# Small half-array matmuls of a group issued in one piece, and gated linear attention with two states

## The chip, the cores and the metric

The kernel runs on 1 core of one Trainium2 chip. TensorE (PE in the views) multiplies matrices from SBUF into banks of PSUM, VectorE (DVE) and ScalarE (ACT) work on SBUF and PSUM, GpSimd (POOL) on SBUF, and SyncE (SP) issues transfers. The metric is the time of one execution on the device, in microseconds.

## The reference, cut to what matters

Four post-norm blocks, whose mixer is chunked softmax attention (layers 0 and 3, 16 heads of 64), gated linear attention (layer 1) and differential attention (layer 2), each followed by a SwiGLU feed-forward network; then a second network with a feed-forward part, a mixer of top-k attention, a short convolution and gates, a memory cross-attention and another feed-forward part. 256 tokens, width 1024, float32. The change touches the products of queries and keys, and this part of the gated linear attention (chunks of 64 tokens, 4 heads, a state of 128 x 256 for each):

```
chunk_kv = jnp.einsum('bnchk,bnchv->bnhkv', k_dec, v)
chunk_decay = jnp.exp(total[:, :, 0]).astype(chunk_kv.dtype)

def step(state, inp):
    dec, kv = inp
    state = dec[..., None] * state + kv
    return state, state
...
_, states = lax.scan(step, init, (jnp.moveaxis(chunk_decay, 1, 0), jnp.moveaxis(chunk_kv, 1, 0)))
o = jnp.einsum('bnchk,nbhkv->bnchv', q, states)
```

## The kernel before

The 256 tokens are two token tiles of 128. Each tile is a generator (`stream`) that goes through the whole network; `run` interleaves the two, tile 1 some quarters of a weight unit behind tile 0. Weights (345 MB) come from DRAM in the order of use, in quarters, and each quarter is split by ScalarE (L268) and VectorE (L269) into two float32r halves, `wh` and `wl`. A product of activations and weights is then three float32r matmuls of 128 x 512 for each row tile (`mm3`, L280, L282, L284, into banks `lin` or `acc`). These are called ordinary matmuls below. Both tiles use the same quarters, so that one tile's weight matmuls can stand on TensorE where the other waits.

The small products are plain float32 matmuls, each of which the trace shows as two records. Some of them use half of the array:

- L574 in `attn_probs`: scores of four heads with 64 features each. Heads with e = 0 lie on partitions 0 to 63 and write to the first of two `at` banks, those with e = 1 lie on partitions 64 to 127 and write to the second. Tile 0 has 128 keys (128 columns), tile 1 has 256. Two such groups ("sub" 0 and 1) belong to each call of the loop over g, 14 groups to each tile in all.
- L842 in `mixer2`: index scores, in the same way; eight matmuls for tile 0, two groups of four for tile 1.
- L741 in `mixer_gla`: keys times values for each chunk c of 64 tokens (partitions 64c and up) and head x of a pair, into `at` bank c.
- L753 in `mixer_gla`: queries of chunk c times the state; 128 rows of the array but 64 columns, so that chunk 0 uses one half of the columns and chunk 1 the other; both write to one bank `lin`.

Behind an L574 group VectorE forms four maxima with the bias (L580), ScalarE four exponentials (L585), TensorE transposes them (L599) into `at` banks, and copies (L606, L608) free these. There are only two `at` banks; all transposes of activations (L326) pass through them too. The state S of the linear attention is one tile, updated in place by VectorE (L749 for the first chunk, L751 then).

The order of issue on each engine is not that of the code. `order_issue` plays the instructions through a list scheduler (`plan_order`, `play`) with assumed durations (`_duration`) and deadlines, and hands the order that it found to the framework as edges; waits follow from the data. So any change of the program gives a new order for all engines.

Of the kernel before, what the change touches and what calls it, by code (L numbers as in the profile page):

```python
# [15 lines left out]
OP = mybir.AluOpType  # L16
# [12 lines left out]
TW = 384          # length of a Toeplitz table  # L29
TREP = 32         # copies of a table in DRAM, for the skewed reads  # L30

LAG = 6           # quarters of a weight unit by which token tile 1 trails token tile 0
LAG0, LAGK = 2, 4   # the lag starts at LAG0 and grows by one every LAGK quarters
WB, RB = 10, 5    # buffers for split and for raw weight quarters
DMAQ = 1          # quarters of 1024 floats in one transfer
AHEAD = 1         # quarters split ahead of token tile 0


# [1 line left out]
# A unit is (key, kind, source, spec). kind "in": eight row tiles of the listed column ranges;  # L40
# kind "out": up to four row tiles of all 1024 columns.
# [74 lines left out]
class Unit:  # L116
    def __init__(self, key, kind, width, nrt):
        self.key, self.kind, self.width, self.nrt = key, kind, width, nrt
        self.cols = nrt * width                      # floats of a partition
        self.per = 2 if kind == "in" else 1          # row tiles of a quarter  # L120
        if kind == "in" and width < 64:
            self.per = 8
        self.nq = nrt // self.per
        self.qcols = self.per * width
        self.dma_q = max(1, min(self.nq, 1024 * DMAQ // self.qcols))   # quarters of one transfer

# [17 lines left out]
def pack_weights(inputs):  # L144
    """The weights in the order of their use: a block for each transfer, whole per partition."""
# [22 lines left out]
def rel_bias_rows(inputs):  # L168
    """[layers, heads, 257], by ascending (key - query)."""
    return np.ascontiguousarray(np.asarray(inputs["a_rel_bias"])[:, ::-1, :].transpose(0, 2, 1))  # L170


# [31 lines left out]
def bcast(ap, n):  # L204
    """A row of n floats in DRAM, read by every partition."""
# [3 lines left out]
class Net:  # L209
    def __init__(self, ctx, tc, A, out):  # L210
# [12 lines left out]
        self.tag_of, self.bufs_of = {}, {}  # L223

    # ---- tiles
# [15 lines left out]

    def bank(self, tag):
        return self.named(self.ps, tag, [128, 512], F32, {"acc": 4, "lin": 2, "at": 2}[tag])

    # ---- weights
# [27 lines left out]
    def pieces(self, n):  # L273
        """The very first quarter comes in two pieces, so that the tensor engine starts on the first."""
# [11 lines left out]
    def lin(self, st, key):  # L286
        """A step for each quarter: [128 tokens, width] = x @ columns of the unit."""
# [12 lines left out]
    def lin_out(self, gt, key, accs, first, last):  # L300
        u = self.by_key[key]
        both = 0 if u is self.units[-1] else u.nq - 1 if last else u.nq       # the quarters that do both halves at once
# [18 lines left out]
    # ---- small pieces  # L321
    def transpose4(self, src, n=4):
        """[128, n*128] -> a bank with [128, n, 128], each block transposed."""
# [33 lines left out]
    # ---- set-up  # L357
# [18 lines left out]
    def setup_later(self):  # L376
# [12 lines left out]
        # w_g2 with b_g as one more row  # L389
# [16 lines left out]
    def setup_last(self):  # L406
# [9 lines left out]
        # -(e1 - e2 + init) = e2 - (e1 + init)  # L416
# [7 lines left out]
    def toeplitz(self, i, bank=None):  # L424
        """Copies of layer i's biases by (key - query), per head, in DRAM."""
# [13 lines left out]
    def bias_tile(self, i, h0):  # L439
        """[128 queries, 4 heads, 256 keys] of the Toeplitz bias, masked in its last block."""  # L440
# [14 lines left out]
    # ---- normalisation  # L455
# [31 lines left out]
    def inv_rms(self, ss, n, scale=1.0):  # L487
        """ss: sums of squares [128, m]; -> scale * rsqrt(ss / n + EPS)."""
# [11 lines left out]
    def inv_rms_row(self, halves, half=False):  # L500
        """rsqrt(mean of squares + EPS) over two halves of 512; times 0.5, as 4 under the root, for half."""
# [37 lines left out]
    # ---- feed-forward  # L539
# [24 lines left out]
    # ---- softmax attention for eight heads of 64, in pairs  # L564
    def attn_probs(self, tt, sub, qT, kT, bias):
        """Four heads (pairs 2*sub, 2*sub+1): unnormalised exponentials [128, 4, keys], 1/sums."""
        nc = self.nc
        nk = 128 * (tt + 1)
        banks = [self.bank("at").rearrange("p (a k) -> p a k", a=2) for _ in range(2)]
        for i in range(2):  # L570
# [19 lines left out]
    def transpose_probs(self, tt, P, hs):  # L590
        """P[:, h, keys] for h in hs -> [128 keys, len(hs), key tiles, 128 queries]."""
# [18 lines left out]
    def to_heads(self, tt, acc, dst, scale=1.0):  # L610
        """A bank [128 tokens, 512] -> dst [128 features, 4, 128 tokens]."""
# [77 lines left out]
    # ---- gated linear attention  # L689
    def mixer_gla(self, tt, st, i):  # L690
        nc = self.nc
        # gates: log_sigmoid((x W1) W2 + b), still times 16
# [35 lines left out]
        on = []  # L728
        if tt == 0:
            self.S = self.t("k4", [128, 1032], 2)[:, :1024].rearrange("p (a k) -> p a k", a=4)  # L730
        S = self.S
        for pr in range(2):
# [3 lines left out]
            banks = [self.bank("at").rearrange("p (a k) -> p a k", a=2) for _ in range(2)]  # L736
            for x in range(2):
                hd = 2 * pr + x
                for c in range(2):
                    cs = slice(64 * c, 64 * c + 64)  # L740
                    nc.tensor.matmul(banks[c][:, x], kd[cs, 128 * hd:128 * hd + 128], v[cs, 256 * x:256 * x + 256],  # L741
                                     start=True, stop=True)
            o = self.bank("lin")
            for c in range(2):
                cs = slice(64 * c, 64 * c + 64)
                for x in range(2):
                    hd = 2 * pr + x
                    if tt == 0 and c == 0:
                        nc.vector.tensor_copy(S[:, hd], banks[c][:, x])  # L749
                    else:  # L750
                        nc.vector.scalar_tensor_tensor(S[:, hd], S[:, hd], decay[:, 2 * hd + c:2 * hd + c + 1],  # L751
# [626 lines left out]
```

## Time and profile before

| | |
|---|---|
| median of 3 runs | 1971.57 us (1969.64 to 1972.45) |
| profiled execution, span | 1969.9 us |
| PE busy | 1945.0 us, 99% |
| DVE busy | 1169.3 us, 59% |
| ACT busy | 927.4 us, 47% |
| POOL busy | 48.6 us, 2% |
| mean transfer rate | 175 GB/s |
| granted TensorE clock, mean | 0.998 |

The profiled execution lies inside the range of the runs. Busy time of PE is the union of matmuls that overlap in its pipeline (an ordinary one lasts some 0.4 us, but the next starts earlier), so what a matmul occupies is read from the distance of starts. The stage of the linear attention's products lies at 370 to 421 us, those of the three softmax layers around 30 to 115, 665 to 750 and 978 to 1063 us, and the mixer of the second network at 1510 to 1575 us.

### The profile page before, as it was taken

The numbers are of one execution on the slowest core, as the hardware profiler recorded it, in microseconds if no ns is written. First come the engines' busy times: TensorE is split into PE (matmuls) and PEld (weight loads), VectorE is DVE, ScalarE is ACT, GpSimd is POOL, SyncE is SP. The second block draws the span as 40 slices with busy tenths as digits, with TensorE's granted clock in tenths as the row PEclk, the third lists the DMA queues.
The fourth block names the chain that finished last, engine by engine and source line by source line (L and its number), as shares of the span: only waits on it lengthen the run. The fifth ranks groups of instructions, "written<-read, shape, count | busy, mean of one in ns | idle before, by whom it ended". The sixth has DMA issues, their size and how long they took to land.

```text
span 1969.9 us, 23888 instructions
## 1 busy us (share of the span) xinstructions
PE 1945.0 (99%) x8998; PEld 1546.9 (79%) x8998; DVE 1169.3 (59%) x1687; ACT 927.4 (47%) x1332; POOL 48.6 (2%) x71
## 2 busy tenths in 40 slices
PE   8999999999999999999999999999999999999998
PEld 6788887678888777888877888878887788788886
DVE  5566456557555768545755655664467857556454
ACT  5445445444444555444554444444444545555442
POOL 0000000000000000000000000000001000000000
PEclk9999999999999999999999999999999999999999
DMA  9436555645555434655543655465545355536562
GB/s 287 150 139 209 181 191 154 193 148 198 186 183 182 171 129 162 222 183 181 183 143 135 217 186 184 150 225 181 186 171 183 113 197 193 163 116 206 180 186 70
DMA packets 103293, 345.59 MB, mean 175 GB/s; under 512 B 13369, under 2 KB 20473, under 8 KB 103178
## 3 DMA queue, kind: packets, MB, share of 16 engines
q1 hardware_dynamic: 103178, 344.07, 51.7%
q8 instruction: 70, 1.15, 0.2%
q14 instruction: 45, 0.37, 0.1%
HBM read 341.01 MB, written 3.01 MB: 175 GB/s over the span
## 4 chain that ended last, share of the span: by engine, by line
PE 95%; DMA 2%; DVE 1%; ACT 1%; issue 0%; SPq 0%; DVEq 0%; POOLq 0%; ACTq 0%
PE lin L282 19%; PE lin L280 19%; PE lin L284 19%; PE acc L282 9%; PE acc L284 9%; PE acc L280 9%; PE at L326 4%; PE at L574 2%; PE lin L662 1%; PE at L599 1%; DMA raw<-in_weights_dram 1%; DMA toep<-t 1%; PE lin L753 0%; PE at L741 0%; PE lin L951 0%; DVE wl L269 0%
## 5 line engine op out<-in xcount | busy, mean ns | idle before, releaser
L269 DVE TENSOR_TENSOR wl<-raw,wh 128x1024 fp32r<-128x1024 f32 (+2 forms) x614 | 741.8, 1216 | 459.6 <-ACT wh L268 459.0
L268 ACT ACTIVATE wh<-raw 128x1024 fp32r<-128x1024 f32 (+2 forms) x614 | 644.7, 1053 | 680.9 <-PE lin L284 437.6
L280 PE MATMUL lin<-wh,sth 128*128 128x512 f32 x1696 | 677.1, 403 | 3.2 <-ACT sth L331 1.4
L282 PE MATMUL lin<-wl,sth 128*128 128x512 f32 x1696 | 671.5, 400 | 1.7 <-DVE wl L269 1.7
L284 PE MATMUL lin<-wh,stl 128*128 128x512 f32 x1696 | 669.1, 399 | 0.0
L280 PEld LDWEIGHTS lin<-wh,sth 128*128 128x128 f32 x1696 | 319.5, 188 | 78.7 <-issue 4.0
L284 PEld LDWEIGHTS lin<-wh,stl 128*128 128x128 f32 x1696 | 319.3, 188 | 77.5 <-issue 4.9
L282 PEld LDWEIGHTS lin<-wl,sth 128*128 128x128 f32 x1696 | 319.4, 189 | 76.8 <-issue 4.8
L282 PE MATMUL acc<-wl,gth 128*128 128x512 f32 x752 | 251.7, 401 | 0.1
L280 PE MATMUL acc<-wh,gth 128*128 128x512 f32 x752 | 248.5, 399 | 0.2 <-ACT gth L331 0.2
L284 PE MATMUL acc<-wh,gtl 128*128 128x512 f32 x752 | 248.3, 398 | 0.0
L284 PEld LDWEIGHTS acc<-wh,gtl 128*128 128x128 f32 x752 | 141.2, 188 | 33.7 <-issue 1.3
L282 PEld LDWEIGHTS acc<-wl,gth 128*128 128x128 f32 x752 | 140.8, 189 | 32.5 <-issue 1.4
L280 PEld LDWEIGHTS acc<-wh,gth 128*128 128x128 f32 x752 | 139.8, 188 | 31.9 <-issue 1.0
L326 PE MATMUL at<-ident,t 128*128 128x128 f32 x604 | 100.4, 273 | 4.5 <-DVE t L534 1.5
L326 PEld LDWEIGHTS at<-ident,t 128*128 128x128 f32 x604 | 75.2, 140 | 28.3 <-ACT t L613 4.1
L331 ACT ACTIVATE gth<-at 128x512 fp32r<-128x512 f32 (+1 forms) x98 | 55.4, 566 | 65.8 <-PE at L326 65.7
L555 DVE TENSOR_TENSOR t<-t,lin 128x512 f32<-128x512 f32 x60 | 41.2, 687 | 74.7 <-PE lin L284 74.7
L347 POOL TENSOR_TENSOR sm<-sm,mhalf 128x1 f32<-128x1 f32 (+2 forms) x42 | 35.8, 852 | 1672.6 <-DVE sm L474 952.1
L332 DVE TENSOR_TENSOR gtl<-at,gth 128x512 fp32r<-128x512 f32 (+1 forms) x98 | 64.1, 654 | 20.2 <-ACT gth L331 17.0
L585 ACT ACTIVATE p<-p,sm 128x128 f32<-128x128 f32 (+1 forms) x112 | 49.6, 444 | 52.4 <-DVE sm L583 52.4
L552 ACT ACTIVATE t<-lin 128x512 f32<-128x512 f32 x60 | 35.9, 598 | 49.8 <-PE lin L284 49.5
(158 smaller groups left out, 911.2 us busy)
## 6 DMA issues: line engine op xcount, KB each, us to landing
raw<-in_weights_dram SPq DMA_DIRECT2D x607, 512.0 KB, 3.5
b<-toep SPq DMA_DIRECT2D x40, 128.0 KB, 4.1
bc<-in_ln_g_dram SPq DMA_DIRECT2D x8, 512.0 KB, 3.7
bc<-in_ln_b_dram SPq DMA_DIRECT2D x8, 512.0 KB, 5.9
toep<-t SPq DMA_DIRECT2D x2, 768.0 KB, 10.4
bc<-in_ffn_post_g_dram SPq DMA_DIRECT2D x2, 512.0 KB, 3.6
p<-in_mem_dram SPq DMA_DIRECT2D x2, 512.0 KB, 6.6
out_dram<-h SPq DMA_DIRECT2D x4, 256.0 KB, 2.0
```

What stands on the lines that cost most here:

```text
L268: nc.scalar.activation(hi[:, c], src[:, c], AF.Copy)
L269: nc.vector.tensor_sub(lo[:, c], src[:, c], hi[:, c].bitcast(F32))
L280: nc.tensor.matmul(o, xh, w, start=first, stop=False)
L282: nc.tensor.matmul(o, xh, w, start=False, stop=False)
L284: nc.tensor.matmul(o, xl, w, start=False, stop=last)
L326: self.nc.tensor.transpose(b[:, k], src[:, k * 128:(k + 1) * 128], self.ident)
L331: self.nc.scalar.activation(hi, b[:, :n], AF.Copy)
L332: self.nc.vector.tensor_sub(lo, b[:, :n], hi.bitcast(F32))
L552: nc.scalar.activation(gate[j], acc, AF.Silu)
L555: nc.vector.tensor_mul(s, s, acc)
L574: nc.tensor.matmul(banks[e][:, i, :nk], qT[ps, pr, :], kT(ps, pr, nk), start=True, stop=True)
L585: nc.scalar.activation(P[:, hh, :nk], P[:, hh, :nk], AF.Exp, bias=nm[:, hh:hh + 1], accum_out=sm[:, hh:hh + 1])
```

## The change

Comments and docstrings are dropped, so that line numbers move (L574 becomes L581, L599 L606, L741 L750, L753 L766, L842 L856, L896 L910, L280, L282 and L284 become L286, L288 and L290). Two things change.

The first: the matmuls of a group are named as a burst. The planner makes the first of a burst wait for everything that any of them needs, all banks of the burst included, lets no other matmul in between, takes the least deadline of the group for all, and assumes a shorter duration for each. Within a group the loops of the code alternate the halves.

The second: the linear attention keeps two state tiles, S[0] for even and S[1] for odd chunks. VectorE writes S[c] from S[1 - c] instead of in place, all four updates of a pair of heads come first, and then the four matmuls with the queries as one burst.

```
+    def burst(self, *banks):
+        self.bursts.append([b.tensor.name for b in banks])
...
         banks = [self.bank("at").rearrange("p (a k) -> p a k", a=2) for _ in range(2)]
+        self.burst(*banks)
...
+            self.S = [self.t("k4", [128, 1032], 2)[:, :1024].rearrange("p (a k) -> p a k", a=4) for _ in range(2)]
...
+            for x in range(2):
+                hd = 2 * pr + x
+                for c in range(2):
+                    if tt == 0 and c == 0:
+                        nc.vector.tensor_copy(S[0][:, hd], banks[c][:, x])
+                    else:
+                        nc.vector.scalar_tensor_tensor(S[c][:, hd], S[1 - c][:, hd], decay[:, 2 * hd + c:2 * hd + c + 1],
+                                                       banks[c][:, x], op0=OP.mult, op1=OP.add)
             o = self.bank("lin")
-            for c in range(2):
-                cs = slice(64 * c, 64 * c + 64)
-                for x in range(2):
-                    hd = 2 * pr + x
-                    if tt == 0 and c == 0:
-                        nc.vector.tensor_copy(S[:, hd], banks[c][:, x])
-                    else:
-                        nc.vector.scalar_tensor_tensor(S[:, hd], S[:, hd], decay[:, 2 * hd + c:2 * hd + c + 1],
-                                                       banks[c][:, x], op0=OP.mult, op1=OP.add)
-                    nc.tensor.matmul(o[cs, 256 * x:256 * x + 256], qT[:, hd, cs], S[:, hd], start=True, stop=True)
+            self.burst(o)
+            for x in range(2):
+                hd = 2 * pr + x
+                for c in range(2):
+                    cs = slice(64 * c, 64 * c + 64)
+                    nc.tensor.matmul(o[cs, 256 * x:256 * x + 256], qT[:, hd, cs], S[c][:, hd], start=True, stop=True)
...
+        if burst:
+            rep = 2.4
         return rep * max(n / 2.4, 40.0) + 3
...
+    for names in bursts:
+        seq = sorted({i for name in names for i, _ in writers[name] if ops[i].eng == "PE"})
+        head = ops[seq[0]]
+        for i in seq:
+            op = ops[i]
+            op.burst = seq
+            op.dur = _duration(op.inst, op.eng, True)
+            if op is not head:
+                for j, full in op.preds.items():
+                    if j not in seq:
+                        assert j < head.idx
+                        head.preds[j] = max(full, head.preds.get(j, 0))
+                op.preds.setdefault(head.idx, 0)
+                head.opens += op.opens
+                op.opens = []
...
+        if op.burst and op.idx == op.burst[0]:
+            d = min(ops[i].dl for i in op.burst)
+            for i in op.burst:
+                ops[i].dl = d
...
+        if lock and op.eng == "PE" and op.idx != lock[0]:
+            return inf
...
+        if lock and e == "PE":
+            lock.pop(0)
+        elif op.burst:
+            lock = op.burst[1:]
```

TensorE's order in the linear attention, tile 0, first pair of heads, before:

```order
L741 MATMUL at_2996<-v_641_2994,p_578_2686 128x256 x2
L280 MATMUL lin_2951<-wh_2745,sth_600_2786 128x512
L282 MATMUL lin_2951<-wl_2746,sth_600_2786 128x512
L741 MATMUL at_2997<-v_641_2994,p_578_2686 128x256 x2
L753 MATMUL lin_3002<-k_626_2918,pt_623_2909 64x256
L284 MATMUL lin_2951<-wh_2745,stl_601_2787 128x512
L753 MATMUL lin_3002<-k_626_2918,pt_623_2909 64x256
L280 MATMUL lin_2951<-wh_2765,sth_600_2786 128x512
L753 MATMUL lin_3002<-k_626_2918,pt_623_2909 64x256
L282 MATMUL lin_2951<-wl_2766,sth_600_2786 128x512
L753 MATMUL lin_3002<-k_626_2918,pt_623_2909 64x256
```

The same place after (k_626 and k_627 are the two states, at_2997 and at_2998 the banks of the two chunks):

```order
L750 MATMUL at_2997<-v_642_2995,p_578_2686 128x256
L750 MATMUL at_2998<-v_642_2995,p_578_2686 128x256
L750 MATMUL at_2997<-v_642_2995,p_578_2686 128x256
L750 MATMUL at_2998<-v_642_2995,p_578_2686 128x256
L286 MATMUL lin_2952<-wh_2745,sth_600_2786 128x512
...
L290 MATMUL lin_2952<-wh_2765,stl_601_2787 128x512
L766 MATMUL lin_3007<-k_626_2918,pt_623_2909 64x256
L766 MATMUL lin_3007<-k_627_2919,pt_623_2909 64x256
L766 MATMUL lin_3007<-k_626_2918,pt_623_2909 64x256
L766 MATMUL lin_3007<-k_627_2919,pt_623_2909 64x256
```

Six pieces have become two, with nine ordinary matmuls between them.

TensorE's order in layer 3, tile 1, the second group of the last heads (p_1829 are the probabilities of the first group), before:

```order
L599 MATMUL at_8434<-ident_82,p_1829_8412 128x128 x2
L284 MATMUL acc_8365<-wh_8387,gtl_1709_7910 128x512
L599 MATMUL at_8434<-ident_82,p_1829_8412 128x128 x2
L574 MATMUL at_8440<-k_1748_8069,q_1824_8397 128x256 x2
L284 MATMUL acc_8366<-wh_8387,gtl_1709_7910 128x512
L280 MATMUL lin_8474<-wh_8263,sth_1655_7673 128x512
L574 MATMUL at_8441<-k_1748_8069,q_1824_8397 128x256 x2
```

And after:

```order
L606 MATMUL at_8435<-ident_82,p_1830_8413 128x128 x2
L286 MATMUL lin_8475<-wh_8264,sth_1656_7674 128x512
L288 MATMUL lin_8475<-wl_8265,sth_1656_7674 128x512
L290 MATMUL lin_8475<-wh_8264,stl_1657_7675 128x512
L286 MATMUL lin_8475<-wh_8264,sth_1656_7674 128x512
L288 MATMUL lin_8475<-wl_8265,sth_1656_7674 128x512
L290 MATMUL lin_8475<-wh_8264,stl_1657_7675 128x512
L581 MATMUL at_8441<-k_1749_8070,q_1825_8398 128x256
L581 MATMUL at_8442<-k_1749_8070,q_1825_8398 128x256
L581 MATMUL at_8441<-k_1749_8070,q_1825_8398 128x256
L581 MATMUL at_8442<-k_1749_8070,q_1825_8398 128x256
```

The first half no longer stands right behind the transposes; the whole group stands six ordinary matmuls later.

TensorE's order in the second network's mixer, tile 0, second group, after (L910 is the 64-column product of probabilities and values, p_2681 the probabilities of the group):

```order
L286 MATMUL acc_12328<-wh_12349,gth_2626_12109 128x512
L581 MATMUL at_12299<-k_2567_11848,q_2668_12264 128x128
L581 MATMUL at_12300<-k_2567_11848,q_2668_12264 128x128
L581 MATMUL at_12299<-k_2567_11848,q_2668_12264 128x128
L581 MATMUL at_12300<-k_2567_11848,q_2668_12264 128x128
L910 MATMUL lin_12574<-va_11844,pt_2677_12292 128x64 x4
L606 MATMUL at_12321<-ident_82,p_2681_12305 128x128
```

Before, three ordinary matmuls and the same four 64-column ones stood between the last half of this group and the first transpose.

## Rows read from the trace of the kernel before

**Rows 1.** The page: span, busy time, and the chain that ended last.

```profile
span 1969.9 us, 23888 instructions
PE 1945.0 (99%) x8998; PEld 1546.9 (79%) x8998; DVE 1169.3 (59%) x1687; ACT 927.4 (47%) x1332; POOL 48.6 (2%) x71
...
PE 95%; DMA 2%; DVE 1%; ACT 1%; issue 0%; SPq 0%; DVEq 0%; POOLq 0%; ACTq 0%
```

**Rows 2.** Groups by line and form: count | busy us, mean ns | idle before.

```profile
L269 DVE TENSOR_TENSOR wl<-raw,wh 128x1024 fp32r<-128x1024 f32 (+2 forms) x614 | 741.8, 1216 | 459.6 <-ACT wh L268 459.0
...
L574 PE MATMUL at<-k,q 64*128 64x256 f32 x112 | 25.1, 405 | 0.5 <-DVE q L608 0.5
...
L574 PE MATMUL at<-k,q 64*128 64x128 f32 x112 | 16.5, 302 | 0.0
L753 PE MATMUL lin<-k,pt 128*64 128x256 f32 x32 | 9.5, 398 | 0.0
L741 PE MATMUL at<-v,p 64*128 64x256 f32 x32 | 8.9, 409 | 0.7 <-ACT v L606 0.7
```

**Rows 3.** Timeline of PE, a whole 256-column group: start us, us, what.

```profile
1052.59 0.40 PE L282 MATMUL acc<-wl,gth 128*128 128x512 f32 x1
1052.91 1.14 PE L574 MATMUL at<-k,q 64*128 64x256 f32 x8
1053.99 0.51 PE L282 MATMUL acc<-wl,gth 128*128 128x512 f32 x1
1054.33 0.63 PE L284 MATMUL acc<-wh,gtl 128*128 128x512 f32 x2
```

**Rows 4.** Timeline of PE, the last half of a 256-column group.

```profile
1059.89 0.40 PE L280 MATMUL lin<-wh,sth 128*128 128x512 f32 x1
1060.21 1.13 PE L574 MATMUL at<-k,q 64*128 64x256 f32 x4
1061.27 0.50 PE L282 MATMUL lin<-wl,sth 128*128 128x512 f32 x1
1061.61 0.39 PE L284 MATMUL lin<-wh,stl 128*128 128x512 f32 x1
```

**Rows 5.** Timeline of PE, a whole 128-column group.

```profile
1028.76 0.39 PE L282 MATMUL lin<-wl,sth 128*128 128x512 f32 x1
1028.99 0.40 PE L284 MATMUL lin<-wh,stl 128*128 128x512 f32 x1
1029.32 0.72 PE L574 MATMUL at<-k,q 64*128 64x128 f32 x8
...
1030.31 0.40 PE L282 MATMUL lin<-wl,sth 128*128 128x512 f32 x1
```

**Rows 6.** Waits of PE, the largest behind the first loads: total us, times, longest us.

```profile
PE at L599 <- ACT p L585: 2.3, 1, 2.3
```

**Rows 7.** Timeline of PE, the first and the last of the 74 places.

```profile
31.90 0.72 PE L574 MATMUL at<-k,q 64*128 64x128 f32 x8
...
1568.83 1.13 PE L574 MATMUL at<-k,q 64*128 64x256 f32 x4
```

**Rows 8.** Timeline of PE, pieces of two and four records on column halves.

```profile
372.78 0.65 PE L753 MATMUL lin<-k,pt 128*64 128x256 f32 x2
...
391.64 1.08 PE L753 MATMUL lin<-k,pt 128*64 128x256 f32 x4
```

**Rows 9.** One stretch (busy us, records, engine by engine), and a group's row there.

```profile
1510.00:1575.00 65.00, 62.67 (x314) 47.05 (x313) 58.44 (x161) 32.89 (x64) 5.61 (x5) 1.00 0.45 146
...
1559.01 1.72 PE L574 MATMUL at<-k,q 64*128 64x256 f32 x8 [0.45 <-DVE q L608]
```

**Rows 10.** DVE: a maximum (timeline), state updates (tile k: ns min/median/max).

```profile
1061.38 0.42 DVE L580 CUSTOM_DVE_ANT_0 p<-at,b 128x256 f32<-128x256 f32 x1 [0.94 <-PE at L574]
...
L751 DVE SCALAR_TENSOR_TENSOR k<-k,sm,at x12: 470/480/481, 373.5 to 419.5; 128x256 f32<-128x256 f32 x12
L749 DVE COPY k<-at x4: 414/418/425, 371.2 to 389.3; 128x256 f32<-128x256 f32 x4
```

More of the change, by code (lines that the diff above doesn't have):

```diff
@@ L223, in __init__ @@
         self.tag_of, self.bufs_of = {}, {}
+        self.bursts = []
     def t(self, tag, shape, bufs, dt=F32):
@@ L729, in mixer_gla @@
         if tt == 0:
-            self.S = self.t("k4", [128, 1032], 2)[:, :1024].rearrange("p (a k) -> p a k", a=4)
+            self.S = [self.t("k4", [128, 1032], 2)[:, :1024].rearrange("p (a k) -> p a k", a=4) for _ in range(2)]
         S = self.S
@@ L736, in mixer_gla @@
             banks = [self.bank("at").rearrange("p (a k) -> p a k", a=2) for _ in range(2)]
+            self.burst(*banks)
             for x in range(2):
@@ L838, in mixer2 @@
             banks = [self.bank("at").rearrange("p (a k) -> p a k", a=npr) for _ in range(2)]
+            self.burst(*banks)
             for x in range(npr):
@@ L1041 @@
 class Op:
-    __slots__ = ("inst", "eng", "dur", "fset", "preds", "succs", "opens", "idx", "dl", "npred", "ready", "start", "end")
+    __slots__ = ("inst", "eng", "dur", "fset", "preds", "succs", "opens", "idx", "dl", "npred", "ready", "start", "end",
+                 "burst")
 def _region(o):
@@ L1064, in _elems, with _duration @@
     return n
-def _duration(inst, eng):
+def _duration(inst, eng, burst=False):
     n = _elems(inst.outs[0])
@@ L1100, in _bytes, with plan_order @@
     return n
-def plan_order(insts, tag_of, bufs_of):
+def plan_order(insts, tag_of, bufs_of, bursts):
     ops, last = [], {}
@@ L1112, in plan_order @@
         op.fset = op.fset if op.fset in ("Exp", "Silu", "Ln", "Sigmoid") else ""
+        op.burst = None
         op.dur = _duration(inst, op.eng)
@@ L1211, in play @@
     turn = {tag: 0 for tag in slots}
+    lock = []
     def eff(op):
         t = op.ready
+        if lock and op.eng == "PE" and op.idx != lock[0]:
+            return inf
+        seen = {}
         for name in op.opens:
-            if place[name] != turn[tag_of[name]]:
+            tag = tag_of[name]
+            if place[name] != turn[tag] + seen.get(tag, 0):
                 return inf
+            seen[tag] = seen.get(tag, 0) + 1
         if op.opens:
@@ L1300, in play, with order_issue @@
     return max(op.end for op in ops), order, opens
-def order_issue(tc, nc, tag_of, bufs_of, rounds=4):
+def order_issue(tc, nc, tag_of, bufs_of, bursts, rounds=4):
     insts = [i for i in nc.all_instructions() if i.is_tile_traced and len(i.outs) and
@@ L1306, in order_issue @@
              and type(i).__name__ not in ("BassTilePoolBoundary", "InstRegisterMove")]
-    ops, users = plan_order(insts, tag_of, bufs_of)
+    ops, users = plan_order(insts, tag_of, bufs_of, bursts)
     t, nominal = 0.0, {}
@@ L1342, in kernel_body @@
     net.run()
-    order_issue(tc, tc.nc, net.tag_of, net.bufs_of)
+    order_issue(tc, tc.nc, net.tag_of, net.bufs_of, net.bursts)
 _DIRECT = [
```

## The prediction, made before the changed kernel was run

> **What bounds the kernel now.** I read the page first: TensorE (PE) is busy 99% of a span of 1969.9 us, and the chain that ended last lies 95% on PE [rows 1]. A busy PE says little by itself, because matmuls overlap; what a matmul costs is the distance from its start to the next start. So the second view was the timeline of PE, and it gives three prices. An ordinary 512-column matmul starts 0.23 us after the one before it (1028.76 to 1028.99) [rows 5]; over all pairs the median is 0.233. Small matmuls on half the array cost more than their own time: each entry into such a stretch and each exit from it delays the neighbours. A whole group of 4 (8 records, since each fp32 matmul is two) starts at 1052.91, PE's next matmul at 1053.99, and from the 512 before to the second 512 behind it is 1054.33 - 1052.59 = 1.74 us [rows 3]. Two ordinary matmuls of that are 0.47; the group costs **1.27 us**, of which 1.08 lies between its start and the next start and 0.19 in entry and exit. A half of such a group (2 matmuls on one bank) costs 1061.61 - 1059.89 - 0.47 = **1.25 us** [rows 4]: as much as the whole. So a group in two halves costs 2.51, because the two halves of the array work at the same time only if both banks' matmuls stand together. With 128 columns a whole group costs 1030.31 - 1028.99 - 0.47 = **0.85** [rows 5].
>
> The third view, groups by line and form, counts what there is: 112 records of L574 with 256 columns and 112 with 128, 32 each of L741 and L753 [rows 2]. The waits of PE come fourth: behind the first loads the longest sum is 2.3 us, one wait at L599 [rows 6]. PE is short of time, not of work, so time taken off PE should come off the span.
>
> **The change part by part.** *What it costs now.* I made the same subtraction, start against start and without the idle time, at all 74 places where these lines stand in the trace, from 31.90 to 1568.83 [rows 7]: L574 with 256 columns 28.2 us, with 128 columns 19.4, L741 9.6, L753 10.6, and L842 of token tile 1 3.1 (that of tile 0 is one piece before and after); in all 70.9. The order confirms it. Of the 14 groups of L574 in tile 1, six stand whole (6 x 1.27), one is whole in the order but its second bank came late (x8 in 1.72 us at 1559.01 [rows 9], about 1.9), four stand in two halves (4 x 2.51) and three in a half and two singles (about 2.9 each): 28.3.
>
> *What it costs after.* The order of the changed kernel has each group in one piece: 14 groups of L574 with 256 columns, 14 with 128, four each of L741 and L753, two of L842. At the price of a whole group:
> - L574: 14 x 1.27 = 17.8 (gain 10.4) and 14 x 0.85 = 11.9 (gain 7.5);
> - L741: 4 x 1.27 = 5.1 (gain 4.5);
> - L842, tile 1: 2 x 1.27 = 2.5 (gain 0.6);
> - L753, unknown: here the halves are halves of the array's columns, and no row has two different ones beside each other. Lower bound 4 x 1.27 = 5.1, as for halves of the rows (gain 5.5). Upper bound without any overlap: a piece of two records lasts 0.65 and one of four 1.08 [rows 8], so eight last 1.08 + 2 x 0.43 = 1.94, which is 0.80 more than the 1.14 of the overlapping eight; 2.07 a group, four groups 8.3 (gain 2.3). I take the lower bound, since the nearest rows are those of L574 and L741: of the same 256 columns, and with the same duration in pieces of one half (1.13 for four records of L574 [rows 4], 1.08 here).
>
> The Trainium skill (TensorE: Matmul & The Clock Gate, Part 3: Packing small matmuls) says that column tiles overlap within about 5 ns of what row tiles do, measured with 32-column tiles. No row here can show it; by it L753 lies at the lower bound, and the sum is the one that I take; without it, at the upper bound, 3.2 us less is gained.
>
> Sum: 10.4 + 7.5 + 4.5 + 0.6 + 5.5 = **28.5 us** of PE time.
>
> *The alternation by itself* I cost at nothing: the whole group at 1052.91 stands in the old order with bank 1 twice and then bank 2 twice, and its eight records still fit into 1.14 us [rows 3], while those whose second bank was late took 1.72 [rows 9]. What counts is that both banks are ready and that nothing stands between.
>
> *The wait for both banks.* Behind a waiting head all of PE waits. In an attention group the half on bank 2 had to wait for that bank before as well, and it was the last to end: 1060.21, next start 1061.27 [rows 4]. A whole group that starts when bank 2 comes free ends at the same time, because it takes as long as that half. What is later are the maxima of the two heads on bank 1 (L580), which VectorE (DVE) could do in the meantime: two operations of 0.42 us for 256 columns [rows 10]. The cover, PE's work between the group and the transposes of its probabilities (L599), is in the new order some ten ordinary matmuls (2.3 us) in most places, as before. Cost taken: 0; bound: if 0.7 us came through at each of the 14 second groups, 10 us.
>
> *Two states.* The same 16 DVE operations are left, but none has to wait until a matmul has read the old state. Four of them now stand between the L741 group and the L753 group: two copies of 0.42 us and two updates of 0.48 (tile 1: four updates), at most 1.9 [rows 10]. Between the groups PE has 9 to 12 ordinary matmuls, 2.1 to 2.8 us. Cost 0; if a weight split (1.2 us on DVE [rows 2]) gets in front, up to 1 us at four places. The second state takes the other of two buffers that layer 0's keys left long before.
>
> *The stage where the gain may not arrive.* From 1510 to 1575 us DVE is busy 58.4 of 65 us [rows 9], with the top-k selection and the weight splits; PE already waited there. The groups in it save 3.5 us of the sum above, and the new order has thin cover: behind the second L574 group of tile 0 only four 64-column matmuls stand before the first transpose that needs its maxima and exponentials, where three ordinary matmuls (0.7 us) more stood behind the group's last half. I take 3 us of the 3.5 as lost; the bounds are nothing lost and all of it.
>
> Everything else is ordered anew too, with as many instructions; L326's transposes stand in 257 runs where they stood in 248, which I leave at nothing. That gives 28.5 - 3 = 25.5. The profiled execution's span is 1969.9, the median of the runs 1971.6, 0.1% apart; taken off the median, **1946 us**.
>
> **The rivals.** *Column halves don't overlap:* 3.2 us less, 1949. For it: no row shows the overlap, and every record of L753 streams through all 128 rows, so two at a time would share them. Against: in pieces of one half the records last as long as those of the row halves.
>
> *The waits come through:* part of the gain turns into waits for softmax chains and for DVE, at the second groups (up to 10 us) and in the linear attention (up to 4): 1952 to 1960. For it: PE's waits were small because its order was fitted to the old pieces, and chains are no shorter now. Against: only one wait of L599 for its exponentials is seen [rows 6], and the other token tile's work lies in between.
>
> *Slower:* the head that waits for both banks. If each of the 39 groups held PE up for 28.5 / 39 = 0.73 us more than now, nothing is left; at 1.0 us each the time is 1982. For it: behind the head stands all of PE, weight matmuls that could run included. Against: the old second half had to wait for the same bank, and the order places ordinary matmuls (six in the place shown) between the last transposes and the group.
>
> *The change does nothing:* the halves already overlapped in hardware where they stood together; if pieces were cheap the gain would be nil. The 1.25 us of a half against 1.27 of a whole speaks against it directly.
>
> **How the numbers follow.** My forecast, overlapping columns and most waits hidden: 0.57, 1940 to 1948. No column overlap: 0.21, 1949. Waits come through: 0.12. No change: 0.04; slower: 0.04; a luckier order than this, below 1940: 0.02. The range from 1938 to 1957 takes the first two whole and half of the third. A measurement of this kernel can tell about 0.2%, 4 us. Faster 0.92, same 0.04, slower 0.04.
>
> **What would show it.** Right: L574, L741, L842 each in runs of 8 records (16 for tile 0 of L842) of about 1.14 us for 256 columns and 0.72 for 128; L753 in runs of 8 that last 1.1 us (overlap) or 1.9 (none); PE's idle time as before, some us more between 1500 and 1570. Wrong: PE waiting at the first matmul of groups for DVE or ScalarE copies, long waits at L599, or runs of 8 that last 1.7 us.

## The result, and the profile after

The changed kernel takes 1948.1 us (median of 4 runs, 1946.5 to 1950.96); the kernel before took 1971.4 beside it (1969.6 to 1972.5). The ratio is 0.9883, 95% interval 0.9868 to 0.9899. The forecast was 1946, with a range of 1938 to 1957: the time is in the range, 2 us above the number. How much of that is understanding and how much is two errors that cancel is told below.

The page of the changed kernel (answers to [rows 1]): span, busy time, and the chain that ended last.

```profile
span 1946.1 us, 23881 instructions
...
PE 1918.8 (99%) x8998; PEld 1535.1 (79%) x8998; DVE 1168.2 (60%) x1687; ACT 926.6 (48%) x1332; POOL 48.5 (2%) x71
...
PE 94%; DVE 3%; DMA 2%; ACT 1%; issue 0%; POOL 0%; SPq 0%; DVEq 0%; POOLq 0%; ACTq 0%
```

PE has the same 8998 matmuls and is busy 26.2 us less (1945.0 - 1918.8), while span minus busy time went from 24.9 to 27.3 us. So the gain is PE time, and part of it came back as waits: DVE's share of the chain went from 1% to 3%.

Groups by line and form of the changed kernel (answers to [rows 2]): count | busy us, mean ns | idle before.

```profile
L581 PE MATMUL at<-k,q 64*128 64x256 f32 x112 | 16.5, 403 | 0.6 <-DVE q L615 0.6
L581 PE MATMUL at<-k,q 64*128 64x128 f32 x112 | 10.0, 297 | 0.0
L750 PE MATMUL at<-v,p 64*128 64x256 f32 x32 | 4.5, 402 | 0.7 <-ACT v L613 0.7
L766 PE MATMUL lin<-k,pt 128*64 128x256 f32 x32 | 4.3, 392 | 0.0
```

The mean of one record is unchanged (403 ns against 405, 392 against 398), the busy time of all is far smaller (16.5 against 25.1, 4.3 against 9.5). The matmuls did not get faster; more of them run at the same time.

Timeline of PE, changed kernel, the group whose halves are halves of the array's columns: start us, us, what.

```profile
360.65 0.40 PE L288 MATMUL lin<-wl,sth 128*128 128x512 f32 x1
360.88 0.39 PE L290 MATMUL lin<-wh,stl 128*128 128x512 f32 x1
361.20 1.08 PE L766 MATMUL lin<-k,pt 128*64 128x256 f32 x8
362.22 0.50 PE L286 MATMUL lin<-wh,sth 128*128 128x512 f32 x1
362.55 0.39 PE L288 MATMUL lin<-wl,sth 128*128 128x512 f32 x1
```

Eight records last 1.08 us, as long as four did [rows 8]: column halves overlap. From 360.88 to 362.55 are 1.67 us; without two ordinary matmuls (0.47) the group costs 1.20. The Trainium skill (TensorE: Matmul & The Clock Gate, Part 3: Packing small matmuls) says that column tiles overlap like row tiles; the trace agrees, with 1.02 us to the next start for halves of 64 columns, against 1.06 to 1.08 for row halves.

**Where the time went, stage by stage.** Below I cut each trace at the same ordinary matmuls (the records of 512 columns, counted from the first) and take the distance of their starts, in us; layer 0 begins with PE's first matmul, and "all the rest" is what else lies between that and the last ordinary one. Each column is one profiled execution. "Small" is the PE time of the small groups in the stage, by the prediction's subtraction; "idle" is PE's.

| stage (ordinary matmuls) | before | changed | difference | small | idle |
|---|---|---|---|---|---|
| layer 0 (1 to 400) | 142.0 | 133.0 | -9.0 | -5.6 | -1.6 |
| linear attention (1200 to 1600) | 124.6 | 112.1 | -12.5 | -10.3 | -2.0 |
| layer 2 (2400 to 2800) | 125.7 | 128.2 | +2.5 | -5.2 | +3.2 |
| layer 3 (3600 to 4000) | 127.9 | 123.1 | -4.8 | -4.3 | 0.0 |
| second network's mixer (5600 to 6000) | 124.3 | 123.2 | -1.1 | -3.0 | +2.2 |
| all the rest | 1314.9 | 1315.9 | +1.0 | 0.0 | +0.6 |

The small groups cost 72.2 us before and 43.7 after (here with the 1.3 us of tile 0's index scores, the same in both): 28.5 us less, the forecast's sum. Not all of the rest belongs to the change. Of layer 0's 9.0 us, 0.5 stand ahead of the 40th ordinary matmul, in the program's start, and 1.7 (0.05 x 35) are a lower clock that the profiled execution of before met behind its wait of 2.28 us at L599 and that of the changed kernel did not meet there. Window of the kernel before (the number ahead of the last two is the granted clock, 1.00 being full speed):

```profile
30.00:65.00 35.00, 32.72 (x161) 24.14 (x160) 21.11 (x55) 19.12 (x43) 0.91 (x3) 0.95 0.94 280
```

And layer 2 became slower. There the chain from the squares to the scaled outputs holds up PE:

Timeline of PE, changed kernel, layer 2, tile 0's outputs.

```profile
664.00 0.47 PE L290 MATMUL lin<-wh,stl 128*128 128x512 f32 x1
666.29 0.50 PE L286 MATMUL lin<-wh,sth 128*128 128x512 f32 x1 [1.81 <-DVE t L680]
...
668.96 0.63 PE L288 MATMUL lin<-wl,sth 128*128 128x512 f32 x1
669.39 0.63 PE L290 MATMUL lin<-wh,stl 128*128 128x512 f32 x1
```

Timeline of DVE, the same place.

```profile
663.61 0.17 DVE L498 TENSOR_SCALAR sm<-sm 128x4 f32<-128x4 f32 x1 [0.26 <-ACT t L676]
664.91 0.17 DVE L502 TENSOR_SCALAR sm<-sm 128x4 f32<-128x4 f32 x1 [1.13 <-POOL sm L353]
665.11 1.12 DVE L680 SCALAR_TENSOR_TENSOR t<-lin,sm,cst 128x128 f32<-128x128 f32 x4
```

Windows of the changed kernel (the granted clock stands where it did above).

```profile
660.00:664.00 4.00, 4.00 (x23) 3.27 (x22) 3.52 (x5) 3.07 (x11) 0.14 (x1) 1.00 0.49 153
664.00:668.00 4.00, 2.19 (x14) 1.62 (x13) 2.42 (x6) 2.95 (x5) 0.88 (x1) 0.91 0.67 241
668.00:675.00 7.00, 7.00 (x30) 5.10 (x30) 4.13 (x12) 2.33 (x6) 0.00 (x0) 0.81 0.46 152
...
746.00:752.00 6.00, 6.00 (x25) 4.88 (x24) 4.57 (x7) 2.26 (x3) 0.00 (x0) 0.73 0.11 33
```

The matmul at 666.29 opens a `lin` bank that L680 frees when it has read it; before it stand a power on POOL (the 1.13 us that L502 waits) and the four scalings. The wait is 1.81 us, and then comes a second price: the granted clock is 1.00 ahead of it, 0.91 and then 0.81 in the next two stretches, and ordinary matmuls stand 0.43 us apart (668.96 to 669.39) where they stand 0.233 at the full clock. That is the lower of the clock's two levels, 1.2 GHz. Around 743 to 745 it happens again, with waits of 0.52, 0.24 and 0.69 us in a row and 0.73 behind them. Apart from the small groups and the idle time, PE's work in this stage cost 4.5 us more than before. The clock of the three windows makes up 3.3 of that (0.09 x 4 + 0.19 x 7 + 0.27 x 6), as much as the idle time itself rose.

Timeline of PE, changed kernel, the second network's mixer.

```profile
1528.07 0.71 PE L581 MATMUL at<-k,q 64*128 64x128 f32 x8
...
1530.53 0.33 PE L606 MATMUL at<-ident,p 128*128 128x128 f32 x1 [0.71 <-ACT p L592]
...
1535.06 1.72 PE L581 MATMUL at<-k,q 64*128 64x256 f32 x8 [0.61 <-DVE q L615]
...
1539.58 0.50 PE L288 MATMUL acc<-wl,gth 128*128 128x512 f32 x1 [1.68 <-DVE wl L275]
```

Timeline of DVE, the copy and the product that free the two `at` banks which the group at 1535.06 takes.

```profile
1534.32 0.68 DVE L615 COPY q<-at 128x512 f32<-128x512 f32 x1
1534.92 0.67 DVE L880 TENSOR_TENSOR v<-v,at 128x512 f32<-128x512 f32 x1
```

The first row of L606 is the place with thin cover that the prediction named: 0.71 us. The group at 1535.06 shows that "once both banks are free" holds in the planner alone. On the chip each matmul waits for its own bank: the first started when L615 had freed its bank, those of the other half stood until L880 ended at 1535.59, and the group took 1.72 us, as the late one of before did [rows 9].

### The profile page after: what moved, and what is told of

The parts are those of the page before. It is cut to its first block, busy times and chain, and to the rows that moved or that the text cites. A ratio compares the mean times of both kernels' runs of the same rounds, so it can differ in the third digit from the quotient of the medians.

```text
span 1946.1 us, 23881 instructions
## 1 busy us (share of the span) xinstructions
PE 1918.8 (99%) x8998; PEld 1535.1 (79%) x8998; DVE 1168.2 (60%) x1687; ACT 926.6 (48%) x1332; POOL 48.5 (2%) x71
## 4 chain that ended last, share of the span: by engine, by line
PE 94%; DVE 3%; DMA 2%; ACT 1%; issue 0%; POOL 0%; SPq 0%; DVEq 0%; POOLq 0%; ACTq 0%
PE lin L286 20%; PE lin L288 19%; PE lin L290 19%; PE acc L288 9%; PE acc L286 9%; PE acc L290 9%; PE at L332 4%; PE lin L669 1%; PE at L581 1%; PE at L606 1%; DVE wl L275 1%; DMA raw<-in_weights_dram 1%; DMA toep<-t 1%; PE lin L965 0%; PE at L953 0%
## 5 line engine op out<-in xcount | busy, mean ns | idle before, releaser
L286 PE MATMUL lin<-wh,sth 128*128 128x512 f32 x1696 | 678.4, 404 | 5.0 <-DVE t L680 1.8
L288 PE MATMUL lin<-wl,sth 128*128 128x512 f32 x1696 | 670.1, 399 | 0.9 <-DVE wl L275 0.9
L290 PE MATMUL lin<-wh,stl 128*128 128x512 f32 x1696 | 670.6, 400 | 0.0
L286 PEld LDWEIGHTS lin<-wh,sth 128*128 128x128 f32 x1696 | 319.6, 189 | 82.2 <-issue 4.4
L290 PEld LDWEIGHTS lin<-wh,stl 128*128 128x128 f32 x1696 | 319.3, 188 | 75.8 <-issue 2.7
L288 PEld LDWEIGHTS lin<-wl,sth 128*128 128x128 f32 x1696 | 319.5, 188 | 72.3 <-DVE wl L275 2.0
L288 PE MATMUL acc<-wl,gth 128*128 128x512 f32 x752 | 252.3, 402 | 2.1 <-DVE wl L275 2.1
L286 PE MATMUL acc<-wh,gth 128*128 128x512 f32 x752 | 249.0, 400 | 0.7 <-ACT gth L337 0.7
L290 PE MATMUL acc<-wh,gtl 128*128 128x512 f32 x752 | 247.9, 398 | 0.0
L288 PEld LDWEIGHTS acc<-wl,gth 128*128 128x128 f32 x752 | 141.3, 189 | 34.8 <-DVE wl L275 3.0
L290 PEld LDWEIGHTS acc<-wh,gtl 128*128 128x128 f32 x752 | 141.7, 189 | 32.6 <-DVE gtl L883 0.3
L286 PEld LDWEIGHTS acc<-wh,gth 128*128 128x128 f32 x752 | 139.9, 188 | 32.5 <-issue 1.6
L338 DVE TENSOR_TENSOR gtl<-at,gth 128x512 fp32r<-128x512 f32 (+1 forms) x98 | 64.1, 654 | 21.4 <-ACT gth L337 18.3
```

What stands on the lines that cost most here:

```text
L286: nc.tensor.matmul(o, xh, w, start=first, stop=False)
L288: nc.tensor.matmul(o, xh, w, start=False, stop=False)
L290: nc.tensor.matmul(o, xl, w, start=False, stop=last)
L338: self.nc.vector.tensor_sub(lo, b[:, :n], hi.bitcast(F32))
```

## The experiments

Theory A throughout: a piece of a small group costs the same whether one half of the array works or both, so what counts is that a group stands in one piece; what was lost was lost to waits of this order and to the clock behind them. Each ratio is to the kernel before, run beside it (its medians were 1971.4 to 1972.8 us), with a 95% interval; the times of stages are those of one profiled execution.

**The alternation alone, and the split alone.** The loops of the four groups are turned (the outer one over the halves):

```
-        for i in range(2):
-            pr = 2 * sub + i
-            for e in range(2):
-                ps = slice(64 * e, 64 * e + 64)
+        for e in range(2):
+            ps = slice(64 * e, 64 * e + 64)
+            for i in range(2):
+                pr = 2 * sub + i
```

> The groups stay in one piece, but each issues its halves one behind the other (first half twice, then second half twice) instead of alternating; the order around them is the changed kernel's in all but some dozens of places. Theory A (what counts is that a group stands in one piece; the alternation costs and brings nothing): a group's 8 records still take 1.08 us to the next start with 256 columns and 0.67 with 128, all small groups together 44 +- 1.5 us of PE, time 1948 +- 4. Rival B (the halves overlap because they alternate): a group takes as long as its two halves one after the other, 2.1 us instead of 1.08 (1.3 instead of 0.67), 38 us more on PE, 1980 to 1986.

1945.9 us (1945.0 to 1950.3), ratio 0.9866 (0.9849 to 0.9884); small groups 44.5 us. Timeline of PE in this run:

```profile
1031.29 0.40 PE L288 MATMUL acc<-wl,gth 128*128 128x512 f32 x1
1031.62 1.14 PE L581 MATMUL at<-k,q 64*128 64x256 f32 x8
1032.69 0.51 PE L288 MATMUL acc<-wl,gth 128*128 128x512 f32 x1
...
1489.88 1.71 PE L856 MATMUL at<-k,q 64*128 64x128 f32 x16
```

A group of four takes 1.07 us to the next start without alternation too; B falls for groups of four. The one place where it shows is L856 of tile 0, where now four matmuls of one half stand ahead of four of the other; in the changed kernel, alternating, its row was

```profile
1489.65 1.16 PE L856 MATMUL at<-k,q 64*128 64x128 f32 x16
```

So 0.55 us: two matmuls in a row on one half still overlap with the two behind them, four do so only in part.

Then, on top of that, one ordinary matmul is put between the halves, in the order that the planner found:

```
+        g = ops[pe[k]].burst
+        if g:
+            n = len(g)
+            nxt = pe[k + n]
+            if "float32r" in str(ops[nxt].inst.ins[0].dtype):
+                pe[k:k + n + 1] = g[:n // 2] + [nxt] + g[n // 2:]
```

> As the run with the halves one behind the other, and in 38 of 39 groups the one ordinary matmul that followed the group stands between its two halves; nothing else differs from that run. Theory A (each piece costs the same whether it holds one half or both): 24 groups of 256 columns cost 2 x 1.25 instead of 1.27 (+1.24 each, 29.8 us), 14 of 128 columns 2 x 0.83 instead of 0.85 (+0.81 each, 11.3 us), together 41 us on PE, of which PE's idle time can take back a few: 1982 to 1990. Rival C (the time fell because the new order is a better one, not because of the pieces): 1946 to 1956.

1984.6 us (1982.3 to 1985.3), ratio 1.0056 (1.0041 to 1.0071), 38.7 us above the run without the split. The small groups cost 82.6 us, 38.1 more. Timeline of PE, one group:

```profile
1065.53 0.40 PE L290 MATMUL lin<-wh,stl 128*128 128x512 f32 x1
1065.86 1.13 PE L581 MATMUL at<-k,q 64*128 64x256 f32 x4
1066.92 0.49 PE L286 MATMUL acc<-wh,gth 128*128 128x512 f32 x1
1067.34 1.13 PE L581 MATMUL at<-k,q 64*128 64x256 f32 x4
1068.40 0.51 PE L286 MATMUL acc<-wh,gth 128*128 128x512 f32 x1
1068.74 0.62 PE L288 MATMUL acc<-wl,gth 128*128 128x512 f32 x2
```

One matmul that only changed places costs its group a second 1.13 us. With an otherwise equal order the time goes past that of the kernel before, whose groups were not all split: this settles A against C.

**The two parts of the change.** One state, updated in place as before, all other groups as changed:

```
-                        nc.vector.scalar_tensor_tensor(S[c][:, hd], S[1 - c][:, hd], decay[:, 2 * hd + c:2 * hd + c + 1],
-                                                       banks[c][:, x], op0=OP.mult, op1=OP.add)
...
-            self.burst(o)
...
+                        nc.vector.scalar_tensor_tensor(S[:, hd], S[:, hd], decay[:, 2 * hd + c:2 * hd + c + 1],
+                                                       banks[c][:, x], op0=OP.mult, op1=OP.add)
+                    nc.tensor.matmul(o[cs, 256 * x:256 * x + 256], qT[:, hd, cs], S[:, hd], start=True, stop=True)
```

> The linear attention updates one state in place as before, and its products with the state are ordered freely; all other groups stay bursts. By the stage's rows the two states brought 10.6 - 4.8 = 5.8 us of the products' PE time and at most the 2 us by which the stage's idle time fell. Theory A: products with the state 10 to 10.6 us again, 1954 to 1956, with 3 us either way for a new order of everything. Rival D (the two states bring nothing by themselves, the gain of that stage is from the keys-times-values bursts): 1948 +- 3.

1956.25 us (1954.3 to 1958.7), ratio 0.9916 (0.9898 to 0.9934). The products with the state cost 11.6 us in pieces, against 4.8. The first two pieces of tile 0's second pair of heads in this run (two records each):

```profile
378.22 0.65 PE L762 MATMUL lin<-k,pt 128*64 128x256 f32 x2
379.22 0.65 PE L762 MATMUL lin<-k,pt 128*64 128x256 f32 x2
```

A, not D: without the second state the matmuls of chunk 1 wait for an update that waits for those of chunk 0, so they can't stand in one piece. The run takes out the second state and the burst that it allows together; two states without that burst were not run.

Bursts in the linear attention alone (the two other calls of `burst` taken out):

```
         banks = [self.bank("at").rearrange("p (a k) -> p a k", a=2) for _ in range(2)]
-        self.burst(*banks)
```

> Bursts and two states in the linear attention alone; scores and index scores are ordered freely as before. The linear attention's stage gave back 12.5 us, the others 11 of their 18 us. Theory A (the stages add up, and what was lost in layer 2 and the second network's mixer came with the bursts there): 1971.4 - 12.5 = 1959 +- 3. Rival E (the waits in layer 2 and the mixer have nothing to do with the bursts and stay): 18.2 us of PE time back on top of 1948, 1966 +- 3.

1960.6 us (1956.9 to 1961.4), ratio 0.9933 (0.9917 to 0.9949). The linear attention's stage takes 112.1 us, as with the whole change, and layer 2 (125.7), layer 3 (127.9) and the mixer (124.3) what they took before. Stages hardly speak to each other, and the loss of layer 2 came with the score groups' bursts: A.

**The luck of an order.** The planner's allowance in deadlines, in the changed kernel and in that of before:

```
-SLACK = 340.0
+SLACK = 380.0
```

> The changed kernel with the planner's allowance in deadlines (SLACK) 380 instead of 340: the same instructions and the same groups in one piece, in another order. It shows how much of a difference the luck of an order makes. Theory A (the time follows the pieces): small groups at 43 to 45 us of PE, 1948 +- 5, with the waits of layer 2 and the mixer changed in place and size. Rival C (the gain is a lucky order): 1955 to 1975.

> The kernel before with the planner's allowance in deadlines (SLACK) 380 instead of 340: the same instructions in another order, groups in as many pieces as that order makes. Theory A: small groups at 68 to 76 us of PE, 1971 +- 6. Rival C (the order of before was an unlucky one): under 1960.

Changed: 1944.15 us (1943.35 to 1946.5), ratio 0.9864 (0.9849 to 0.9878), small groups 43.2. Before: 1970.3 (1969.0 to 1971.1), ratio 0.9990 (0.9981 to 0.9999), small groups 72.3. Other orders move the time by 1 to 4 us; 26 us lie between the two kernels here too.

**Layer 2.** First without bursts in that layer:

```
-                P, ri = self.attn_probs(tt, sub, qT, lambda ps, pr, nk: kT[ps, pr, :nk], bias)
+                P, ri = self.attn_probs(tt, sub, qT, lambda ps, pr, nk: kT[ps, pr, :nk], bias, not diff)
```

> The changed kernel without bursts in layer 2 alone (8 of 28 score groups are ordered freely there). Theory A (layer 2 lost 7.7 us to waits and a lower granted clock that came with the bursts there, against 5.2 us of gain): that stage takes 125.7 us again, with no wait over 0.8 us and the clock at 1.00, 2.5 us less than with bursts: 1945.6 +- 2. Rival E (the waits have to do with the order of everything): the 5.2 us come back and the waits stay, 1953 +- 2.

1947.7 us (1946.3 to 1949.4), ratio 0.9880 (0.9865 to 0.9895). The stage is back at 125.7 us, with 1.7 us of idle time instead of 4.9: what A says of the place. The 2.5 us don't show in the time, because two other stages were longer by as much (layer 0 by 1.1, the stretch ahead of the mixer by 1.7). The second is worth a look. Timeline of PE, this run:

```profile
1458.55 0.40 PE L290 MATMUL lin<-wh,stl 128*128 128x512 f32 x1
1460.48 1.29 PE L332 MATMUL at<-ident,t 128*128 128x128 f32 x8 [1.53 <-DVE t L540]
...
1463.88 0.63 PE L286 MATMUL lin<-wh,sth 128*128 128x512 f32 x1
1464.30 0.63 PE L288 MATMUL lin<-wl,sth 128*128 128x512 f32 x1
```

Timeline of PE, changed kernel, the same instructions:

```profile
1460.49 0.40 PE L290 MATMUL lin<-wh,stl 128*128 128x512 f32 x1
1462.42 1.29 PE L332 MATMUL at<-ident,t 128*128 128x128 f32 x8 [1.53 <-DVE t L540]
...
1465.10 0.39 PE L286 MATMUL lin<-wh,sth 128*128 128x512 f32 x1
1465.33 0.40 PE L288 MATMUL lin<-wl,sth 128*128 128x512 f32 x1
```

The same wait of 1.53 us; behind it the clock fell in one execution (0.42 us between starts) and not in the other (0.23).

Then the planner's durations for PE, set to what the trace shows, first everywhere:

```
         if burst:
-            rep = 2.4
+            return 106.0 + 0.824 * n
+        if n == 512 and rep == 1:
+            return 233.0
```

> The changed kernel, with the planner's durations for TensorE set to what the profile shows: 233 ns for an ordinary matmul (216 before), 317 and 212 ns for a matmul of a group with 256 and 128 columns (259 and 131 before). Theory F (the waits left over stand where the plan runs ahead of TensorE's real time): idle time of PE falls by 2 to 5 us, 1943 to 1946. Rival G (the plan errs in the chains of the other engines, not in TensorE's durations): a new order and no systematic gain, 1948 +- 5.

1950.2 us (1946.2 to 1951.9), ratio 0.9886 (0.9869 to 0.9903): no systematic gain, F falls. But by stages it is far from nothing: layer 2 took 121.6 us, 6.6 less than in the changed kernel and with all its groups whole, and layer 0 took 139.9, 6.9 more (a wait of 3.25 us for exponentials stands there, and the lower clock around it cost another 3.4). So the durations were then measured ones for layer 2's instructions alone (`REAL` holds their names):

```
+        if inst.name in REAL:
+            if burst:
+                return 106.0 + 0.824 * n
+            if n == 512 and rep == 1:
+                return 233.0
```

> The changed kernel, with the measured durations of TensorE (233 ns an ordinary matmul, 317 and 212 ns one of a group) in the planner for layer 2's attention alone; TensorE's order differs from the changed kernel's in rows 2555 to 3194 of 8091 only, all groups stay in one piece. Theory A (what layer 2 lost is this order's waits and the lower clock behind them, not a price of the bursts): the stage takes 121.6 us as in the run with these durations everywhere, instead of 128.2, and the others what they took: 1941.5 +- 2. Rival H (the good stage there came from what lay ahead of it): 128 us again, 1948 +- 2.

1943.0 us (1940.8 to 1946.7), ratio 0.9856 (0.9835 to 0.9876). Layer 2 takes 122.2 us, the other four named stages within 0.1 us of the changed kernel's. Windows of this run:

```profile
664.00:668.00 4.00, 4.00 (x26) 2.95 (x24) 3.13 (x4) 2.99 (x5) 0.00 (x0) 1.00 0.49 179
668.00:675.00 7.00, 7.00 (x35) 5.57 (x32) 4.72 (x17) 3.98 (x10) 0.00 (x0) 1.00 0.48 152
...
746.00:752.00 6.00, 6.00 (x28) 4.87 (x27) 4.73 (x5) 2.34 (x2) 0.00 (x0) 1.00 0.93 290
```

Neither wait is left at those places and the clock stays at 1.00. So what layer 2 lost was the price of the one order that the planner happened to find, not of the bursts: A, not H. Of the 5.2 us that the groups gain there, 3.5 now arrive (122.2 against 125.7 before); PE is still idle 1.4 us more than before, most of it in one new wait of 2.35 us. With both, the allowance of 380 and these durations in layer 2:

> The same with the planner's allowance in deadlines 380 instead of 340. Theory A (stages add up): the run with 380 alone gave 1944.15 with 126.8 us in layer 2; with 121.6 there, 1939 +- 2, the fastest of all. Rival H: 1944 +- 2.

1941.5 us (1937.2 to 1943.0), ratio 0.9839 (0.9820 to 0.9857), the lowest median of all, with 121.9 us in layer 2; it can't be told from the one before by the intervals. Its profiled execution spent 136.9 us in layer 0, where the same order took 133.2 in the run with 380 alone. The difference lies in the program's start: from PE's first matmul to the 40th ordinary one are 19.8 us against 16.2, and from there to the end of the stage 117.0 in both. In this run ordinary matmuls still stood 0.43 us apart at 14 us:

```profile
14.03 0.63 PE L289 MATMUL lin<-wl,sth 128*128 128x512 f32 x1
14.46 0.63 PE L291 MATMUL lin<-wh,stl 128*128 128x512 f32 x1
```

In the other they stood 0.24 apart from 11.65 us on.

**The mixer.** Its score groups without bursts:

```
-            P, ri = self.attn_probs(tt, sub, qT, lambda ps, pr, nk: kT[ps, 0, :nk], lambda pr, e: mask)
+            P, ri = self.attn_probs(tt, sub, qT, lambda ps, pr, nk: kT[ps, 0, :nk], lambda pr, e: mask, False)
```

> The changed kernel without bursts for the four score groups of the second network's mixer. TensorE's order differs from the changed kernel's only there. Theory A (of 3.05 us that the groups gain in that stage, waits take back 2.2): 0.9 +- 0.5 us slower in the stage's rows, 1949 +- 2, not to be told from the changed kernel by the times. Rival I (as predicted, the waits take back all): the stage is as long or shorter without the bursts, 1947 +- 2.

1947.7 us (1946.4 to 1949.2), ratio 0.9874 (0.9858 to 0.9889). In the stage the groups cost 2.4 us more and PE is idle 2.3 less; it lasts 123.6 us, 0.4 more than with bursts. That lies between A and I, and no run here can tell them apart: the four groups' gain there is taken back by waits but for a few tenths. The two waits left in the stretch are these:

```profile
1522.44 0.73 PE L288 MATMUL acc<-wl,gth 128*128 128x512 f32 x2 [0.54 <-DVE wl L275]
...
1537.50 0.50 PE L288 MATMUL lin<-wl,sth 128*128 128x512 f32 x1 [1.00 <-DVE wl L275]
```

L606 no longer waits for its exponentials. A side result: TensorE's order in layer 2 is the changed kernel's in this run, and so is the idle time there (4.9 us), yet the stage took 126.6 us instead of 128.2. The 1.5 us are ordinary matmuls, so the clock again: behind the wait at 666 us, 1.84 us here, it did not fall. Neither run's order nor its waits explain that.

## Why the prediction came out, and which of its steps did not

**The sum of pieces** held. Forecast and measured after, in us: L574/L581 with 256 columns 17.8 and 18.3, with 128 columns 11.9 and 11.7, L741/L750 5.1 and 5.1, L842/L856 of tile 1 2.5 and 2.5, L753/L766 5.1 and 4.8; the gain of all 28.5 and 28.5. The split run shows the cause, not only the sum: cutting 38 groups in two costs 38.1 us of PE and 38.7 us of time.

**Column halves** lay at the lower bound that I took: 1.02 us from start to next start for eight records.

**The alternation at nothing:** right for groups of four, where the run without it was no slower. It is worth 0.55 us where four matmuls of one half would stand in a row, which the change did not touch.

**The wait for both banks at nothing:** right: PE's idle time ahead of the groups is 1.3 us in all, where it was 1.5. Nor does the chip wait for both banks; it waits bank by bank, as the group at 1535.06 shows, the one of 39 that stood apart for it (1.72 us).

**Two states at nothing:** right. With their burst they remove the pieces (5.8 us). The stage's idle time fell by another 2.0, from 2.6 to 0.7, but that is not theirs: it is 0.7 in the run with one state too, and 0.8 in the kernel before with the allowance of 380. It is the order's.

**The mixer's stage:** I took 3 of its 3.5 us as lost. It gained 3.0, and 2.2 came back as idle time, 0.7 of it at the place named. Right in kind, 0.8 too much.

**The step that failed** is "Everything else is ordered anew too [...], which I leave at nothing". It was not nothing: layer 2 lost 7.7 us against its sum (3.2 idle, 4.5 in the rest of PE's work, 3.3 of them by the lower clock), while layer 0 and the linear attention gained 3.4 and 2.2 beyond theirs and layer 3 0.5; the rest of the program lost 1.0. That is 8.7 lost and 6.1 gained outside the terms of the sum, and with the mixer's 1.9 the net of 4.5 us by which the traces' stages fall short of the 28.5; I had 3. The sum of the pieces is understood; that the rest came so close is luck, since errors of both signs stand in it. The prediction's rival "the waits come through" put these waits at L599 (now L606), for the exponentials of the second groups. In layer 2 they came at another chain, squares to power to scaled outputs, which holds a `lin` bank; and their second price, the clock, was in no case of mine, though the trace of before shows it behind the very wait of 2.3 us that I read for [rows 6].

**Slower** is excluded by the result itself, **no change** by it and by the split run: the same groups with each half in a piece of its own take 1985 us.

**What stays open:** how much of layer 0's extra gain belongs to the change. Its stage took 132.9 to 136.9 us in the kernels with whole score groups there and the changed kernel's durations in the planner, and 141.1 to 142.0 in those without. Behind the 40th ordinary matmul, and without the 1.7 us of lower clock that two of the latter met, that is 115.9 to 117.4 against 122.5 to 123.5 us: 5.1 to 7.6 less, around the 5.6 of the sum. So an extra gain there isn't shown. Open too is when the clock falls behind a wait.

## What to carry to other kernels

Price a small matmul on half of the array by the piece, from the last ordinary matmul before it to the second one behind, and keep both halves of a group next to each other: the second half is then nearly free, in either order. Look for what forbids that in the data, such as a state updated in place, and give it a second buffer. When an edit lets a scheduler order everything anew, allow some us of either sign for each stage with long chains, and read the result by stage: a stage that lost can be ordered again by itself and the gain of the others kept.

## What the hardware showed that I had not expected

A wait of PE can cost twice. After 1.81 us of waiting in layer 2 ordinary matmuls stood 0.43 us apart instead of 0.233. In the 13 traces the clock fell 14 times between the program's start and its end, each time during a wait of PE or less than 2 us behind one. But most waits have no such price, and it isn't a matter of the wait's length alone. The wait of 1.53 us that stands in twelve of the traces was followed by a fall in two of them: the same instructions ran at the full clock in one execution and had five starts 0.43 to 0.47 us apart in another, which cost that stretch 1.6 us more, and in the run with measured durations in layer 2 the clock stayed at 1.00 behind this wait:

```profile
681.59 0.50 PE L287 MATMUL lin<-wh,sth 128*128 128x512 f32 x1 [2.35 <-ACT t L621]
```

The Trainium skill (TensorE: Matmul & The Clock Gate, Part 1: The HAM clock gate) says that the gate watches activity in a rhythm that runs on its own and doesn't start with the kernel; these runs agree in that equal orders met it differently. Executions of one kernel differ by it: of 13 of the kernel before, run beside the orders with the allowance of 380, the three with a mean clock of 1.000 spanned 1966.7 to 1968.0 us, the five with 0.996 or 0.997 1971.7 to 1974.3 (0.003 of the span are 6 us).

The halves need not alternate to run side by side, up to a point: with the order half 1, half 1, half 2, half 2 the second half's records still ran beside the first's (1.14 us for eight), but with four and four in line only in part (1.71 us for sixteen, 1.16 when they alternate).
